# A chunked delta-rule recurrence inside a decoder trunk: inverting blocks of 32 tokens on VectorE instead of 16 on GpSimd

## The chip, the core and the metric

The kernel runs on one core of a Trainium2 chip. A core has five engines that run side by side, each with its own queue of instructions in program order: TensorE (PE, matmuls, with weight loads shown apart as PEld), VectorE (DVE), ScalarE (ACT), GpSimd (POOL) and SyncE (SP, which here issues all DMAs). They meet through semaphores. SBUF is the working memory of 128 partitions, PSUM the memory that matmuls write to. The metric is the time of one execution in microseconds on the device.

## What is computed

Two layers of a decoder trunk over 512 tokens of width 1024. In each layer one projection of x feeds four branches (a recurrence, causal attention, a convolution, cross-attention to a memory); each branch is gated, projected by its own w_o, merged under sigmoid gates, and a layer norm ends the layer. The change is in the recurrence (RWKV-7, 8 heads of 64):

```python
p = p + mu * (p_prev - p)
r, k, v, wl, al = jnp.split(p, (W, 2 * W, 3 * W, 3 * W + RWKV_LORA), axis=-1)
w_log = -jax.nn.softplus(-(w0 + jnp.tanh(wl) @ w2)) - 0.5
decay = jnp.exp(-jnp.exp(w_log.astype(jnp.float32)))
a = jax.nn.sigmoid(a0 + al @ a2)
...
def step(state, inp):
    r_t, w_t, k_t, v_t, a_t, b_t = inp        # a_t = -kk, b_t = kk * a
    sa = jnp.einsum('bhvk,bhk->bhv', state, a_t)
    state = (state * w_t[:, :, None, :] + sa[..., None] * b_t[:, :, None, :]
             + v_t[..., None] * k_t[:, :, None, :])
    return state, jnp.einsum('bhvk,bhk->bhv', state, r_t)
```

## The kernel before

**An order made ahead.** The class Plan keeps estimated clocks for the engines and lets generators ("tasks") take turns: a main stream of projections (weights are fetched in blocks of 512 KB, split by ScalarE and VectorE into a high and a low part, and multiplied in three passes) and side tasks, of which the recurrence's units are some. A task that yields "pe", "small", "late" or "ride" asks for a turn on TensorE; "small" and "late" collect work on 64x64 tiles so that TensorE changes its tile size seldom, and "ride" waits up to 4 us (RIDE) for such a visit of somebody else. A task that yields "slack" waits until VectorE's estimated queue is empty. The program is then issued in exactly that order, and every engine runs its own part of it in order. A matmul in float32 shows as two records in the trace.

**The recurrence.** A layer has four units (rwkv_unit, L839): two pairs of channel groups j0 times two halves of the tokens. A unit handles 8 chunks of 64 tokens for two heads at a time, on all 128 partitions. Its stages:

- *head* (L852 to L892): waits for `L["mids"] == un`, so that it starts when the unit before has passed its middle. z (decay and a, from the low-rank projections), tanh, the cumulative sum cum, exponentials D and E, and from them bt, kt, AR and w.
- *g* (L894 to L926): 64x64 matmuls that give the triangular matrix M of each chunk, key norms, and the masks' inputs. M is scaled and its four 16x16 diagonal blocks are packed into Mc.
- *substitution* (L931 to L968): Mc goes through DRAM (d1) into W, where each of 64 partitions holds one 16x16 block; GpSimd inverts all of them by 28 products and sums (ZT, tmpW); the result and its transpose go through DRAM (d2) into tc, zc and zq. That is 9 DMAs.
- meanwhile NQ, the bonus (bo, from r, k and v) and token-major copies of bt and kt (tokens, on TensorE); most of them yield "slack".
- *x0, x1, x2* (L1038 to L1104): three visits to 64x64 tiles. With T and Z, the inverted blocks spread to block-diagonal matrices, and M with its diagonal blocks removed (moff), x0 makes P and its transpose PT, x1 makes P·Z and P·P, which become QQ and PP, and x2 multiplies PP and QQ to the inverse Zi of the 64x64 matrix. x2 also holds the product of NQ and vt. A visit x0 also holds 32 other matmuls (x_0x or x_1x in the trace).
- *va, gb* (L1119 to L1164): the chunk's transition matrices Gs, H, B, Y0. `L["mids"]` counts up here.
- *state chain* (L1167 to L1190): three steps w of one product each, which "ride" in visits x0, x1 and x2 of the next unit; then yb, which may share the next unit's va.
- group norm and output.

rkv_items (L1256) puts the projections r, k, v of each channel group into the main stream in the order r0 k0 v0 r1 k1 v1; after v1 the two units of the pair are started.

L259 and L353 are the helpers through which VectorE, ScalarE and GpSimd operations and matmuls are issued, so most rows of the profile bear these lines; rows are told apart by tile names (x stands for x0, x1 and x2, g for g0 and g1). In the main stream ps_* and po are projections of 512 columns; mt and merged are VectorE's readers of po.

Of the kernel before, what the change touches and what calls it, by code (L numbers as in the profile page):

```python
# [10 lines left out]
F32 = mybir.dt.float32  # L11
# [5 lines left out]
ALU = mybir.AluOpType  # L17
# [30 lines left out]
for _n, _c in _PARTS:  # L48
# [6 lines left out]
    ("minc", 64), ("moff", 64), ("m16", 16), ("bm", 4), ("id2", 128),  # L55
# [169 lines left out]
class Engine:  # L225
# [5 lines left out]
    def __getattr__(self, name):  # L231
        f = getattr(self.eng, name)

        def call(*a, **k):
# [3 lines left out]
            for d in (o if name in ("activation", "copy") or self.key == "POOL" else i).shape[1:]:  # L238
                n *= d
# [93 lines left out]
def trunk_kernel(ctx: ExitStack, tc: tile.TileContext, A, out, dbg=None):  # L333
# [87 lines left out]
    scr = [[dp.tile([64 * (n + 1), 256], F32, tag=f"scr{n}{i}", name=f"scr{n}{i}").rearrange("a b -> (a b)") for n in range(2)] for i in range(2)]  # L421
# [24 lines left out]
    def params(l):  # L446
# [10 lines left out]
        om = cp.tile([128, 17], F32, tag="om", name=f"om{l}", bufs=2)  # L457
        V.tensor_scalar(out=om[:, 0:13], in0=prm[:, 0:13], scalar1=-1.0, scalar2=1.0, op0=ALU.mult, op1=ALU.add)
        ka = PCOL["k_a"]
        V.tensor_scalar(out=om[:, 13:17], in0=prm[:, ka:ka + 4], scalar1=-1.0, scalar2=1.0, op0=ALU.mult, op1=ALU.add)  # L460
        PRM[l] = prm, hp, om
# [247 lines left out]
    def layer_items(l):  # L709
# [67 lines left out]
        def begin_rwkv(get):  # L777
# [6 lines left out]
            L["blk"] = [L["rp"].tile([64] + n, F32, tag=x, name=x + t_) for x, n in (("W", [16, 16]), ("ZT", [2, 16, 16]), ("tmpW", [56]))]  # L784
# [11 lines left out]
            plan.spawn(parts())  # L796

# [15 lines left out]
        L["units"] = L["chains"] = L["mids"] = L["subs"] = L["read"] = L["fronts"] = L["backs"] = L["ends"] = 0  # L813
# [20 lines left out]

        def both(ap):

            return ap.rearrange("p s (c w) -> p (s c) w", w=64)

        def rwkv_unit(j0, hf, rkv):  # L839
# [3 lines left out]
            rr, kr, vr = ([x[n][:, cs] for x in rkv] for n in "rkv")  # L843
# [8 lines left out]
            yield lambda: L["mids"] == un  # L852
            th, ta = rk("s0", [2, 256], "th"), rk("s1", [2, 256], "ta")
            for s, j in js:
# [6 lines left out]
                S.activation(ta[:, s], z[:, 1, :], AF.Tanh, scale=0.5, bias=hp("a0", j))  # L861
# [3 lines left out]
            cum, kk, sq = rk("s2", [2, 256], "cum"), rk("s3", [2, 256], "kk"), rk("s5", [2, 256], "sq")  # L865
            for s, j in js:
                V.tensor_tensor_scan(out=cum[:, s], data0=reset, data1=th[:, s], initial=0.0, op0=ALU.mult, op1=ALU.add)
                S.activation(sq[:, s], kr[s], AF.Square, scale=pr("k_k", j))
                S.activation(kk[:, s], kr[s], AF.Copy, scale=pr("k_k", j))
# [4 lines left out]
            dl = rk("dl", [8, 1], bufs=2)  # L874
            S.copy(dl, D[:, :, 64:65])
            E = rk("s0", [2, 256], "E")
            S.activation(E, cum, AF.Exp)
            bt, kt, w = rk("bt", [2, 256]), rk("kt", [2, 256]), rk("s4", [2, 256], "w")
            V.scalar_tensor_tensor(out=bt, in0=ta, scalar=1.0, in1=kk, op0=ALU.add, op1=ALU.mult)
            V.scalar_tensor_tensor(out=bt, in0=bt, scalar=0.5, in1=E, op0=ALU.mult, op1=ALU.mult)  # L880
            for s, j in js:
                S.activation(w[:, s], ta[:, s], AF.Identity, scale=hp("k_a", j), bias=om[:, 13 + j:14 + j])
            yield
            AR = rk("AR", [2, 4, 2, 64])
            V.scalar_tensor_tensor(out=AR.rearrange("p s c m w -> p (s c) m w")[:, :, 0, :], in0=both(kk), scalar=-1.0, in1=D[:, :, 0:64], op0=ALU.mult, op1=ALU.mult)
# [3 lines left out]
            for s in SUB:  # L889
                V.tensor_tensor(out=w[:, s], in0=w[:, s], in1=kr[s], op=ALU.mult)  # L890
            V.tensor_tensor(out=kt, in0=w, in1=E, op=ALU.mult)
            yield  # L892

            g0, g1 = yield from pg.take([128, 2, 512], "g" + t, 2, soon)  # L894
# [26 lines left out]
            Mc = rk("zc", [8, 16], "Mc")  # L921
# [4 lines left out]
            d1, d2 = scr[un % 2]  # L926
            W, ZT, tmp = L["blk"]

            zt = []

            def substitution():  # L931
# [13 lines left out]
                for q in range(1, 15):  # L945
# [5 lines left out]
                    if q % 2:  # L951
                        yield
# [1298 lines left out]
```

## Time and profile before

| | |
|---|---|
| median of 3 runs | 1472.24 us (1472.14 to 1473.07) |
| the profiled execution | 1472.63 us, span 1470.8 us |
| TensorE busy / weight loads busy | 1458.1 us / 1227.7 us |
| VectorE, ScalarE, GpSimd busy | 1041.1, 682.8, 143.3 us |
| granted TensorE clock | 0.998 |

The span runs from the first to the last instruction; the execution's time is 1.8 us longer. Busy times count an instruction from start to end, and matmuls overlap, so TensorE's busy time is not its work; distances between the starts of matmuls are. In a row of a timeline the numbers are start and duration in us, then engine, line, operation, tiles out<-in, the shape and how many records were merged.

### The profile page before, as it was taken

Reading aid. Unit: us, or ns where it says so; the run is one execution under the profiler, and the core shown is the slowest. Engines: PE = TensorE matmul, PEld = TensorE weight load, DVE = VectorE, ACT = ScalarE, POOL = GpSimd, SP = SyncE. Lnnn points to the kernel's source line nnn. Section 1 sums busy time; section 2 is a strip of 40 time slices with the busy share of each in tenths; the row PEclk is TensorE's granted clock in tenths of the full one; section 3 lists DMA queues with packets and bytes.
Section 4 is the critical chain, followed back from the end, with each engine's and each line's share of the span. In section 5 each row is a group of like instructions: output and inputs, shape, how many; then the busy total and the mean of one; then the engine's idle time right before and its main releaser. Section 6 shows DMA issues by size and latency. Waiting matters only on the chain.

```text
span 1470.8 us, 28765 instructions
## 1 busy us (share of the span) xinstructions
PE 1458.1 (99%) x11673; PEld 1227.7 (83%) x11673; DVE 1041.1 (71%) x2025; ACT 682.8 (46%) x1331; POOL 143.3 (10%) x327
## 2 busy tenths in 40 slices
PE   9999999999999999999999999999999999999997
PEld 8888888888888888888999888888878888888886
DVE  6799997785756574655554899987867476756756
ACT  5556654436434444443264456633455444444331
POOL 0000000030201112100010000000030203030003
PEclk9999999999999999999999999999999999999999
DMA  6454333232232323333354152423232314132532
GB/s 220 126 145 105 93 110 99 86 84 95 82 90 81 92 75 97 99 127 125 112 165 123 61 147 68 133 88 101 88 104 61 112 47 126 51 108 90 193 95 83
DMA packets 90025, 154.03 MB, mean 105 GB/s; under 512 B 41634, under 2 KB 48034, under 8 KB 89892
## 3 DMA queue, kind: packets, MB, share of 16 engines
q1 hardware_dynamic: 89892, 152.19, 34.8%
q8 instruction: 92, 1.51, 0.4%
q14 instruction: 41, 0.34, 0.1%
HBM read 134.84 MB, written 5.78 MB: 96 GB/s over the span
## 4 chain that ended last, share of the span: by engine, by line
PE 96%; DVE 2%; ACT 1%; DMA 1%; issue 0%; SPq 0%; DVEq 0%; ACTq 0%
PE ps_m L353 23%; PE po L353 12%; PE pz L353 4%; PE ps_rg L353 3%; PE ps_cg L353 3%; PE ps_xg L353 3%; PE ps_r L353 3%; PE ps_v L353 3%; PE ps_xq L353 3%; PE ps_val L353 3%; PE ps_k L353 3%; PE ps_glu L353 3%; PE ps_mg L353 2%; PE ms L353 2%; PE pl L353 2%; PE x L353 2%
## 5 line engine op out<-in xcount | busy, mean ns | idle before, releaser
L259 DVE SCALAR_TENSOR_TENSOR cacc<-hpad,prm,cacc 128x512 f32<-128x512 f32 x240 | 178.9, 748 | 3.8
L259 ACT ACTIVATE tm<-ps_m,prm 128x512 f32<-128x512 f32 x64 | 44.0, 688 | 160.6 <-PE ps_m L353 160.4
L259 DVE SCALAR_TENSOR_TENSOR mt<-tm,po 128x512 f32<-128x512 f32 x48 | 33.0, 687 | 79.0 <-PE po L353 78.8
L259 POOL TENSOR_TENSOR ZT<-ZT,tmpW 64x14 f32<-64x14 f32 (+6 forms) x112 | 46.3, 413 | 8.8
L259 POOL TENSOR_SCALAR ZT<-W 64x256 f32<-64x256 f32 x8 | 5.7, 718 | 408.3 <-DMA W<-scr 296.0
L259 ACT ACTIVATE mP<-ms,nmm 128x128 f32<-128x128 f32 (+3 forms) x64 | 33.7, 529 | 21.0 <-DVE nmm L259 16.2
L259 POOL TENSOR_TENSOR tmpW<-ZT,W 64x14 f32<-64x14 f32 (+6 forms) x112 | 39.6, 353 | 8.2
L259 DVE TENSOR_TENSOR merged<-merged,mt 128x512 f32<-128x512 f32 x48 | 33.4, 697 | 1.6
L259 POOL MEMSET D<- 128x8 f32 x8 | 0.9, 115 | 336.9 <-DVE mP L259 158.3
L259 DVE CUSTOM_DVE_ANT_0 ms<-ms,causal 128x128 f32<-128x128 f32 (+3 forms) x64 | 31.1, 499 | 0.5 <-PE ms L353 0.2
L259 ACT COPY mPT<-mt 128x128 f32<-128x128 f32 (+3 forms) x64 | 26.4, 428 | 5.2 <-PE mt L358 4.9
L358 PE MATMUL mt<-cst,mP 128*128 128x128 f32 x160 | 26.8, 274 | 0.4 <-ACT mPT L259 0.4
L259 DVE TENSOR_SCALAR mP<-mP,smm 128x128 f32<-128x128 f32 (+3 forms) x64 | 24.8, 387 | 2.4
L358 PEld LDWEIGHTS mt<-cst,mP 128*128 128x128 f32 x160 | 20.2, 140 | 6.8 <-issue 0.9
L259 POOL TENSOR_SCALAR lrs<-lmv 128x1 f32<-128x1 f32 x8 | 4.4, 550 | 220.1 <-DVE lmv L259 215.4
L259 ACT ACTIVATE yb<-yb,mr,gr 128x64 f32<-128x64 f32 x64 | 22.1, 430 | 0.0
L353 PE MATMUL ms<-kTl,qT 96*128 96x128 f32 (+3 forms) x64 | 21.5, 336 | 0.0
L259 DVE SCALAR_TENSOR_TENSOR merged<-tm,po 128x512 f32<-128x512 f32 x16 | 11.0, 686 | 14.0 <-PE po L353 14.0
L259 POOL TENSOR_SCALAR gr<-gm 128x8 f32<-128x8 f32 x8 | 3.2, 396 | 180.6 <-DVE gm L259 180.6
L353 PE MATMUL ms<-kTh,qTl 96*128 96x128 f32 (+3 forms) x64 | 20.6, 322 | 0.0
L353 PE MATMUL ms<-kTh,qT 96*128 96x128 f32 (+3 forms) x64 | 20.5, 321 | 0.0
L259 ACT ACTIVATE xP<-xs,nmx 128x256 f32<-128x256 f32 x32 | 15.2, 474 | 11.2 <-DVE nmx L259 11.2
(3585 smaller groups left out, 5213.0 us busy)
## 6 DMA issues: line engine op xcount, KB each, us to landing
w<-in_w_ch_dram SPq DMA_DIRECT2D x146, 512.0 KB, 3.6
w<-in_w_o_dram SPq DMA_DIRECT2D x32, 512.0 KB, 3.6
w<-in_w_out_dram SPq DMA_DIRECT2D x16, 512.0 KB, 3.5
w<-in_w_lat_dram SPq DMA_DIRECT2D x15, 336.0 KB, 2.9
w<-in_w_mk_dram SPq DMA_DIRECT2D x8, 512.0 KB, 3.5
w<-in_w_mv_dram SPq DMA_DIRECT2D x8, 512.0 KB, 3.9
w<-in_w_qk_dram SPq DMA_DIRECT2D x8, 320.0 KB, 3.5
mr<-in_memT_dram SPq DMA_DIRECT2D x8, 256.0 KB, 5.5
```

Source lines behind the costliest of these rows:

```text
L259: return self.plan.keep(f(*a, **k))
L353: plan.keep(nc.tensor.matmul(o, lhsT, rhs, start=start, stop=stop))
L358: plan.keep(nc.tensor.transpose(o, i, ident))
```

## The change

1. The block that is inverted directly is 32 tokens wide, made of two 16-wide inverses and one product between them. VectorE does it: `solve` inverts the 16x16 blocks in place by doubling (2, 4, 8), then two more products give the off-diagonal 16x16 block (ax, bc). POOL's ZT and tmpW go. The blocks Mo beside the diagonal take their own way through DRAM (dm). The DMAs are twelve instead of nine.
2. moff now removes 32-wide blocks, so one factor is enough: x0 makes PP from M and tt (the transposed inverse, made by a VectorE transpose), 32 columns wide; x1 multiplies PP with Zd and also holds the product of NQ and vt. x2 is gone, with P, PT, Q, QQ and T.
3. The head waits for `L["heads"] == un`, which the unit before sets after its x0, and it stops for `L["mids"] == un` only before kt, sq and AR. Step w of the state chain may go on from the next unit's g (`L["goes"]`), and the second step waits for its x0. w moves to the shared pool u of 32 buffers; kk is not stored, its factors are in om (8 more columns).
4. r and k of both channel groups are projected before v, and the units start after the second k; the bonus and the transposes of v wait for v (`spoken`). Several "slack" yields are gone. Transposes of v come before x0 instead of after it.
5. Setup: two DMAs fill the unused half of a scratch tensor with zeros, and a constant bm2 is added.

The diff's core:

```diff
+            if l == 0:
+                for x in scr:
+                    DMA(rows(x[2])[1], zero)
...
-            yield lambda: L["mids"] == un
-            th, ta = rk("s0", [2, 256], "th"), rk("s1", [2, 256], "ta")
+            yield lambda: L["heads"] == un
+            th, w = rk("PT", [2, 256], "th"), u("w" + t).rearrange("p (s w) -> p s w", s=2)
...
-            V.scalar_tensor_tensor(out=bt, in0=ta, scalar=1.0, in1=kk, op0=ALU.add, op1=ALU.mult)
-            V.scalar_tensor_tensor(out=bt, in0=bt, scalar=0.5, in1=E, op0=ALU.mult, op1=ALU.mult)
+            for s, j in js:
+                V.scalar_tensor_tensor(out=bt[:, s], in0=kr[s], scalar=om[:, 21 + j:22 + j], in1=E[:, s], op0=ALU.mult, op1=ALU.mult)
+            V.scalar_tensor_tensor(out=bt, in0=w, scalar=1.0, in1=bt, op0=ALU.add, op1=ALU.mult)
...
+            yield lambda: L["mids"] == un
+            kt, sq, AR = rk("kt", [2, 256]), rk("s5", [2, 256], "sq"), rk("AR", [2, 4, 2, 64])
+            for s, j in js:
+                V.scalar_tensor_tensor(out=AR[:, s, :, 0, :], in0=kr[s].rearrange("p (c w) -> p c w", c=4), scalar=om[:, 17 + j:18 + j], in1=D[:, 4 * s:4 * s + 4, 0:64], op0=ALU.mult, op1=ALU.mult)
...
+            L["goes"] += 1
...
+            V.tensor_scalar(out=Mo, in0=M8[:, :, 16:32], scalar1=bm[:, 0:1], scalar2=None, op0=ALU.mult)
+            V.scalar_tensor_tensor(out=Mo, in0=M8[:, :, 48:64], scalar=bm[:, 2:3], in1=Mo, op0=ALU.mult, op1=ALU.add)
...
+                for i in range(2):
+                    DMA(W[32 * i:32 * i + 32, 0:256], pairs(d1)[i], f"W{i}" + t)
...
+                yield from solve()
+                plan.due(W)
+                yield
+                DMA(ax[:, 0], W[0:32, 0:256], "a0" + t)
+                DMA(bc[:, 0], W[32:64, 0:256].unsqueeze(1).to_broadcast([32, 4, 256]), "b0" + t)
+                for i, d in enumerate((dl_, dr)):
+                    DMA(pairs(d)[i], W[32 * i:32 * i + 32, 0:256])
...
+                for x, y, c in ((0, 1, 1), (1, 2, 0)):
+                    for i in range(2):
...
+                        V.tensor_tensor(out=pr[i], in0=src.unsqueeze(2).to_broadcast([128, 2, 16, 16]),
+                                        in1=by.unsqueeze(1).to_broadcast([128, 2, 16, 16]), op=ALU.mult)
+                    for i in range(2):
+                        V.tensor_reduce(out=ax[:, y].rearrange("p (r k) -> p r k", k=16)[:, 2 * i:2 * i + 2], in_=pr[i], axis=AX.X, op=ALU.add)
+                    yield
...
+                DMA(rows(dr)[0], ax[:, 2])
...
+                DMA(zq[:, :, 0:16], dl_.rearrange("(e p t) -> p e t", e=8, t=16), "z0" + t)
+                DMA(zq[:, :, 16:32], dr.rearrange("(e p t) -> p e t", e=8, t=16))
...
+            def solve():
+
+                w3 = W[:, 0:256].rearrange("p (r c) -> p r c", c=16)
+                w4 = W.rearrange("p (i x) -> p i x", x=68)
+                V.memset(W[:, 0:256:17], 1.0)
+                t8 = ax[0:64, 2, 0:8].rearrange("p (i c) -> p i c", i=4)
+                for o, x, y in (...):
+                    V.tensor_tensor(out=t8, in0=x.to_broadcast([64, 4, 2]), in1=y.to_broadcast([64, 4, 2]), op=ALU.mult)
+                    V.tensor_tensor(out=o, in0=o, in1=t8, op=ALU.add)
...
+                for n in (4, 8):
...
+                    for step in range(2):
+                        for i, x, y in zip(at, us, ps):
...
+                            V.tensor_tensor(out=y, in0=src.unsqueeze(2).to_broadcast([64, n, n, n]),
+                                            in1=by.rearrange("p k c -> p c k").unsqueeze(1).to_broadcast([64, n, n, n]), op=ALU.mult)
+                        for i, x, y in zip(at, us, ps):
+                            V.tensor_reduce(out=w3[:, i:i + n, i + n:i + 2 * n] if step else x, in_=y, axis=AX.X, op=ALU.add)
...
+                plan.due(Mo)
+                yield
+                DMA(dm.rearrange("(c p t) -> p c t", c=8, t=16), Mo)
+                plan.due(dm)
+                yield
+                DMA(bc[:, 1], pairs(dm)[0].unsqueeze(1).to_broadcast([32, 4, 256]))
...
+            tt = rk("tt", [8, 32])
+            V.transpose(out=tt.rearrange("p e t -> p (e t)"), in_=zq.rearrange("p e t -> p (e t)"))
...
-            for q, a, b in ((0, M, T), (1, T, M)):
-                for s in SUB:
-                    for cp, c2, h in quads:
-                        MM(x0[HALF[h], q, s, c2, cp], a[HALF[c2], s, 2 * h + cp], b[HALF[c2], s, 2 * h + cp], start=True, stop=True, four=True)
+            for s in SUB:
+                for h, cp, c2 in quads:
+                    MM(x0[HALF[c2 ^ cp], c2, 2 * s + h], M[HALF[c2], s, 2 * h + cp], tt[HALF[c2], s, 2 * h + cp], start=True, stop=True, four=True)
...
-            for q, a, b in ((0, P, Zd), (1, PT, P)):
-                for s in SUB:
-                    for cp, c2, h in quads:
-                        MM(x1[...], a[HALF[h], s, 2 * cp + c2], b[HALF[h], s, 2 * cp + c2], start=True, stop=True, four=True)
...
-                    MM(x2[HALF[h], 0, s, c2, cp], PP[HALF[c2], s, 2 * h + cp], QQ[HALF[c2], s, 2 * h + cp], start=True, stop=True, four=True)
+                    MM(xz[HALF[h], s, g, cp], PP[HALF[g], cp, 2 * s + h], Zd[HALF[g], cp, 2 * s + h], start=True, stop=True, four=True)
             for s in SUB:
                 for cp, c2, h in quads:
-                    MM(x2[HALF[h ^ cp], 1, s, c2, h], NQ[s][HALF[c2], 2 * h + cp, 0], vt[s][HALF[c2], 2 * h + cp], start=True, stop=True, four=True)
+                    MM(xq[HALF[h ^ cp], s, c2, h], NQ[s][HALF[c2], 2 * h + cp, 0], vt[s][HALF[c2], 2 * h + cp], start=True, stop=True, four=True)
...
-            yield lambda: L["chains"] == un and (un == 3 or L["fronts"] > un + 1)
+            yield lambda: L["chains"] == un and (un == 3 or L["goes"] > un + 1)
...
+                    if len(states) == 3 - hf and un < 3:
+                        yield lambda: L["fronts"] > un + 1
...
-                    if n == "v" and j % 2:
+                    if n == "k" and j % 2:
                         for hf in range(2):
-                            plan.spawn(rwkv_unit(j - 1, hf, rkv[j - 1:j + 1]))
+                            plan.spawn(rwkv_unit(j0, hf, rkv[j0:j0 + 2]))
...
-            for i, n in enumerate("rkv"):
+            for i, n, j in (0, "r", 0), (1, "k", 0), (0, "r", 1), (1, "k", 1), (2, "v", 0), (2, "v", 1):
```

More of the change, by code (lines that the diff above doesn't have):

```diff
@@ L237, in call @@
             n = 1
-            for d in (o if name in ("activation", "copy") or self.key == "POOL" else i).shape[1:]:
+            for d in (o if name in ("activation", "copy", "memset") or self.key == "POOL" else i).shape[1:]:
                 n *= d
@@ L2074, in layer_items @@
         ch_item(12, "wlal", wlal, lambda: "lora" in L)
-        for j in range(4):
+        for j in (0, 2):
             rkv_items(j)
```

197 lines of the change are left out of this document (103 added, 94 removed).

## The prediction

> **What bounds the kernel now.** I read the page first: busy shares, then the chain that ended last.
>
> ```profile
> PE 1458.1 (99%) x11673; PEld 1227.7 (83%) x11673; DVE 1041.1 (71%) x2025; ACT 682.8 (46%) x1331; POOL 143.3 (10%) x327
> ...
> PE 96%; DVE 2%; ACT 1%; DMA 1%; issue 0%; SPq 0%; DVEq 0%; ACTq 0%
> ```
>
> TensorE (PE) is busy in 99% of the 1470.8 us span, and 96% of the chain is its own queue. A busy share can hide waits, so I went on to the view of who waited for whom, for PE alone.
>
> ```profile
> PE x L353 <- issue: 0.9, 2, 0.5
> ...
> PE bo L353 <- DVE rbl L259: 0.4, 1, 0.4
> PE cqs L353 <- DVE cql L259: 0.4, 1, 0.4
> PE pl L353 <- DVE w2l L259: 0.3, 1, 0.3
> PE pmv L353 <- DVE w124l L259: 0.2, 1, 0.2
> ```
>
> VectorE (DVE) cost PE 0.4 + 0.4 + 0.3 + 0.2 = 1.3 us in the whole run. So the recurrence's latency is covered by other projections, and only what PE itself issues counts. What a visit to the recurrence costs PE is read from start times in the timeline; this is the visit that the change removes (x2 of the first unit):
>
> ```profile
> 347.95 0.39 PE L353 MATMUL ps_m<-xh,w58l 128*128 128x512 f32 x1
> 348.27 0.69 PE L353 MATMUL x<-QQ,PP 64*64 64x64 f32 x32
> 348.78 0.65 PE L353 MATMUL x<-vt,NQ 64*64 64x64 f32 x32
> 349.36 0.50 PE L353 MATMUL po<-yxg0l,w59h 128*128 128x512 f32 x1
> 349.70 0.39 PE L353 MATMUL po<-yxg0h,w59h 128*128 128x512 f32 x1
> ```
>
> The 512-column matmuls start every 0.23 us although each row says 0.39: they overlap, so distances between starts are the price. From 347.95 to 349.70 are 1.75 us, in which two large matmuls (0.23 each) also ran: the visit costs 1.75 - 0.46 = **1.29 us**. Each record x32 is 16 float32 matmuls of two records; two such groups take 2 x 0.47 = 0.94, so going to 64x64 tiles and back costs 0.35.
>
> [...]
>
> **The change, part by part.**
>
> *Factors instead of powers.* With 16-wide blocks a unit needs P and PT (x0), two products with them (x1) and a last product (x2): five groups of 16 matmuls. With 32-wide blocks one factor is left: x0 has one group, now 32 columns wide, and x1 has one group and the NQ.vt group that was in x2. Eight units (four in each of two layers):
>
> ```profile
> L353 PE MATMUL x<-M,T x256: 218/218/218, 340.8 to 1314.9; 64*64 64x64 f32 x128
> ```
>
> 256 records are 8 units of 32. In x0 one group goes; its price between starts:
>
> ```profile
> 340.76 0.65 PE L353 MATMUL x<-M,T 64*64 64x64 f32 x32
> 341.23 0.41 PE L353 MATMUL x_0x<-AR,bt 64*64 64x64 f32 x16
> ```
>
> that is 0.47 us. x1 keeps two groups. x2 goes as a visit, 1.29 us. Per unit 0.47 + 1.29 = 1.76, times eight = **-14.1 us**.
>
> The other x0 group shrinks from 64 to 32 columns. The trace has no 32-column matmul; the nearest rows are 64 columns (0.47) and 1 column:
>
> ```profile
> 296.66 0.59 PE L353 MATMUL g<-cst,sq 64*64 64x1 f32 x32
> 297.10 1.08 PE L353 MATMUL g_0x<-AR,kt 64*64 64x128 f32 x32
> ```
>
> 0.44 us for a group of one column. So between nothing and 8 x 0.03 = 0.2 us is saved; I take nothing. [...] A price in proportion to columns would add 8 x 0.24 = 1.9 us of gain; I keep that for the low end.
>
> *Rides.* State steps w ride in visits of the next unit; with x2 gone they are to ride in g, x0 and x1. One costs, from its start to the large matmul after it:
>
> ```profile
> 1324.20 0.41 PE L353 MATMUL w<-S,Gs 64*64 64x64 f32 x8
> 1324.54 0.50 PE L353 MATMUL ps_rg<-xl,w214h 128*128 128x512 f32 x1
> ```
>
> 0.34 less the return of about 0.1: the same in any visit, so nothing. A step that misses its visit pays one of its own, 0.35. Six of the 18 change their host (three rides in each of six unit pairs, the first now in g): from nothing to 6 x 0.35 = 2.1, or 18 x 0.35 = 6.3 if all miss. I take nothing, since g of the next unit now starts only after the unit's own gb has been read, as the first step does.
>
> *x1 stalls.* A few x1 visits break in the middle:
>
> ```profile
> 345.21 0.46 PE L353 MATMUL x<-P,PT 64*64 64x64 f32 x16 [0.35 <-issue]
> ```
>
> The waits view has 0.9 us of it in all. It may stay or go; I count nothing and keep 0.9 for the low end.
>
> *The inversion moves from GpSimd to VectorE.* No row shows solve() itself; these are the nearest forms:
>
> ```profile
> L259 DVE TENSOR_REDUCE nmx<-xs 128x1 f32<-128x256 f32 x32 | 13.4, 418 | 0.2
> ...
> L259 DVE BATCH_NORM_STATS2 gs<-yb 128x6 f32<-128x64 f32 x64 | 9.2, 210 | 0.0
> ...
> L259 DVE SCALAR_TENSOR_TENSOR Mc<-M,cst,Mc 128x128 f32<-128x128 f32 x24 | 8.4, 352 | 0.8
> ...
> L259 DVE SCALAR_TENSOR_TENSOR w<-r,prm,w 128x256 f32<-128x256 f32 x16 | 7.4, 486 | 0.0
> ...
> L259 DVE TENSOR_TENSOR QQ<-x,Q 128x512 f32<-128x512 f32 x8 | 5.5, 687 | 5.8 <-PE x L353 5.8
> ...
> L259 DVE RECIPROCAL rn<-s 128x4 f32<-128x4 f32 x16 | 1.9, 163 | 0.3
> ```
>
> Removed per unit: T, QQ, PP, one bt, one AR, five operations of 512 at 0.69 = 3.4 us. Added: memset and four tiny ones at 0.16 = 0.8; eight of 64 elements at 0.21 = 1.7; twelve of 512 (products and reductions; a reduction of 256 takes 418 ns, so 512 is near 687) = 8.2; Mo 0.6; two halves each of PP, bt and AR, at 0.42 to 0.49, 2.8; the 32x32 transpose, 256 elements, 0.4. Sum 14.5, **net +11 us per unit, 89 us in the run** (DVE 71% to about 77%). None of it is on PE's chain as long as VectorE still empties PSUM and splits weights in time. The cover:
>
> ```profile
> 280.00:600.00 320.00, 318.79 (x3568) 262.06 (x3567) 207.62 (x396) 145.88 (x287) 56.52 (x139) 1.00 0.30 85
> ```
>
> ```profile
> L259 DVE SCALAR_TENSOR_TENSOR mt<-tm,po 128x512 f32<-128x512 f32 x48 | 33.0, 687 | 79.0 <-PE po L353 78.8
> ```
>
> In layer 0's recurrence VectorE works 207.6 of 320 us; four units add 44, 79%. At the tightest reader, po, it idled 79 us before 48 operations: it came first and waited for PE. A split weight is ready about 10 us ahead:
>
> ```profile
> 321.05 1.23 DVE L259 TENSOR_TENSOR w57l<-w,w57h 128x1024 fp32r<-128x1024 f32 x1
> ...
> 331.75 0.39 PE L353 MATMUL ps_m<-xl,w57h 128*128 128x512 f32 x1
> ```
>
> If the cover fails: solve and the two products queue VectorE work in four runs of 2.5 to 2.8 us per unit, 32 in the run. A po caught behind one is read up to 2.8 + 0.7 us late, and its PSUM buffer is needed 12 x 0.23 = 2.7 us later: 0.7 us of PE per run, at most 32 x 0.7 = 22 us. Bounds 0 and 22. Nearest row: all of today's VectorE waits, 1.3 us; I take as much again, **+1.3**.
>
> *DMAs.* The step issues twelve small DMAs instead of nine on SP's queue, where weights queue too, with one more round trip through DRAM (and two zero fills once). Today's waits there:
>
> ```profile
> SPq L365 <- DVE Mc L259: 83.0, 8, 14.2
> ```
>
> Weights already sat behind waits of up to 14.2 us without PE noticing. VectorE takes POOL's place as the one waited for; below 14 us nothing changes. Cost 0, upper end inside the 22 above.
>
> *Head ahead, r and k ahead of v.* The head begins with its z matmuls:
>
> ```profile
> L353 PEld LDWEIGHTS zw<-lxw,lhw x16: 187/188/188, 279.9 to 1264.1; 128*128 128x128 f32 x16
> ```
>
> From 279.9 to the first g (sq at 296.66, above) are 17 us, which now lie beside the unit before. The z matmuls, bo and the transposes are the same in number; exponentials, cum, bt and w only run earlier, beside the other unit. This shortens the recurrence, not PE's work. Nothing is gained, since PE has no hole at the end of the recurrence; nothing is lost except that VectorE's work is packed closer, which is the risk above. v now comes last: v0 and v1 are 48 matmuls of 0.23, 11 us, less than the first head's 17, so bo's PSUM bank, which is held until v is there, is not held longer. w takes one of the 32 shared buffers per unit; a wait for it could hold ScalarE's tanh and what stands behind it, but a unit ahead there is room: nothing, and at most part of the 22. The removed ScalarE copies (46% busy) and the few setup operations count nothing.
>
> **Sum.** The profiled execution took 1472.63 us (span 1470.8 and 1.8 around it), 0.4 above the median of 1472.24. 1472.6 - 14.1 + 1.3 = 1459.8, so **1460**.
>
> **Rivals.**
> 1. *Rides miss.* Steps or yb make visits of their own: 2.1 to 6.3 us back, 1462 to 1466. For it: the timetable is estimated ahead. Against: the rows quoted above, where they ride.
> 2. *VectorE becomes the bound inside the recurrence* (the slower side). Four units in 320 us are 80 us each; with the head's 17 us gone they are 63, and 207.6 + 44 us of VectorE work have 252 us: full. po is then late after nearly each run: +22, **1480**. It decides from (14.1 + 2.9) / 32 = 0.53 us per run. Against: the idle 79 us at mt, PE's 1.3 us of waits, and that part of the 207.6 belongs to the other projections and shrinks with the stretch.
> 3. *No change*: with weight loads at 83% PE had room and something else sets the pace, so the time stays at 1472; or about half of the 22 us and some missed rides give the gain back. 1470 to 1475.
> 4. *The move up is what counts*: the recurrence's end was what PE waited for, and the 17 us of each head count too, at least in part. Against: the waits view has no such wait. Below 1455.
>
> **How the numbers follow.** Forecast (1455 to 1464) 0.62; missed rides and small VectorE losses (1464 to 1469) 0.14; no change 0.10; slower 0.10; more than forecast 0.04. Low end: 1459.8 less 1.3, 1.9 and 0.9 is 1455.7, so 1455. High end: the 22 us at half, 1459.8 - 1.3 + 11 = 1469.5, and a share of the missed rides, 1471; that leaves out the slower case and the cases below 1455, and part of no change. About 0.2% (2.9 us) is what a measurement of this kernel can tell from no change; so faster 0.80, same 0.10, slower 0.10.
>
> **What would show it.** Right: x falls from 192 records a unit (six rows like the one quoted) to 96; one visit to 64x64 tiles fewer in each unit, with w still riding in the others; PE's VectorE waits under 3 us; DVE near 1130 us; POOL down by the ZT and tmpW rows. Wrong: starts of po more than 0.23 us apart with mt as releaser, w visits alone, or weights late behind SP's new waits.

## The result, and the profile after

| | before | after |
|---|---|---|
| median | 1472.45 us (1472.14 to 1473.07, 4 runs) | 1462.68 us (1461.68 to 1465.0, 4 runs) |
| the profiled execution | 1472.63 us, span 1470.8 | 1465.0 us, span 1463.2 |
| visits to 64x64 tiles, time in them | 51, 101.4 us | 44, 89.1 us |

The ratio is 0.9935, 95% interval [0.9918, 0.9953]: faster by 10 us, with 1460 predicted. The last row of the table was counted over the starts of TensorE's matmuls, as the prediction did for one visit; in the profiled execution of e0, below, it is 44 visits and 87.7 us.

The page of after, its busy shares and its chain:

```profile
PE 1446.8 (99%) x10905; PEld 1218.1 (83%) x10905; DVE 1128.7 (77%) x2261; ACT 672.1 (46%) x1275; POOL 44.9 (3%) x79
...
PE 90%; DVE 5%; ACT 1%; DMA 1%; issue 1%; SPq 0%; DVEq 0%; ACTq 0%
```

TensorE is as busy as before and still the bound, but VectorE has come up to 77%, and its share of the chain from 2% to 5%. The x tiles of after, by tile (count of records, duration, first and last start):

```profile
L353 PE MATMUL x<-tt,M x256: 219/219/241, 324.9 to 1295.9; 64*64 64x32 f32 x128
...
L353 PE MATMUL x<-Zd,PP x256: 218/218/267, 329.3 to 1299.3; 64*64 64x64 f32 x128
...
L353 PE MATMUL x<-vt,NQ x256: 218/218/218, 329.8 to 1299.7; 64*64 64x64 f32 x128
```

Three rows of 256 records are 96 a unit, half of the 192 before. Two visits of the second unit in the timeline (start, duration):

```profile
394.55 0.67 PE L353 MATMUL x<-tt,M 64*64 64x32 f32 x32
395.04 0.44 PE L353 MATMUL x_1x<-AR,bt 64*64 64x64 f32 x16
...
399.28 0.69 PE L353 MATMUL x<-Zd,PP 64*64 64x64 f32 x32
399.80 0.65 PE L353 MATMUL x<-vt,NQ 64*64 64x64 f32 x32
400.26 0.41 PE L353 MATMUL w<-S,Gs 64*64 64x64 f32 x8
400.61 0.50 PE L353 MATMUL ps_r<-xl,w66h 128*128 128x512 f32 x1
```

The group of 32 columns takes 395.04 - 394.55 = 0.49 us, no less than one of 64. The state step w rides in x1, as it was to; all 18 steps found a host.

Who PE waited for in after (total, times, longest, in us):

```profile
PE gb_1x L353 <- issue: 2.1, 1, 2.1
PE bo L353 <- DVE rbl L259: 1.7, 1, 1.7
PE cqs L353 <- DVE cql L259: 1.0, 1, 1.0
PE pl L353 <- ACT xh L259: 1.0, 1, 1.0
PE warm L353 <- PEq L2312: 0.8, 1, 0.8
PE x L353 <- DVE PP L259: 0.6, 1, 0.6
PE mt L358 <- ACT mPT L259: 0.4, 1, 0.4
PE ps_m L353 <- DVE mt L259: 0.4, 1, 0.4
PE pq L353 <- ACT xql L259: 0.3, 1, 0.3
PE ps_r L353 <- DVE mt L259: 0.2, 1, 0.2
PE ps_cg L353 <- DVE mt L259: 0.2, 1, 0.2
```

The waits for VectorE are 1.7 + 1.0 + 0.6 + 0.4 + 0.2 + 0.2 = 4.1 us, against 1.3 before, and more than the under 3 us that the prediction gave as a sign of being right; a hole of 2.1 us in gb_1x waits for nothing that the profile shows. VectorE in after, by form, and its busy time in layer 0's recurrence (the third busy time of the window, whose columns are those of the prediction's window):

```profile
L259 DVE SCALAR_TENSOR_TENSOR mt<-tm,po 128x512 f32<-128x512 f32 x48 | 32.8, 684 | 63.7 <-PE po L353 62.9 <-issue 0.6
L259 DVE TENSOR_TENSOR pr<-ax,bc 128x512 f32<-128x512 f32 x32 | 32.4, 1055 | 0.0
L259 DVE TENSOR_REDUCE ax<-pr 128x32 f32<-128x512 f32 x32 | 20.4, 679 | 0.0
...
L259 DVE TENSOR_TENSOR pw<-ax,W 64x512 f32<-64x512 f32 x8 | 8.4, 1049 | 0.3
```

```profile
280.00:600.00 320.00, 319.36 (x3254) 263.21 (x3253) 257.10 (x543) 143.36 (x267) 10.78 (x17) 1.00 0.33 92
```

VectorE's busy time there rose from 207.62 to 257.10 of 320 us (the third of the bracketed counts is its own: 396 instructions became 543). At the tightest reader, mt, its idle time fell from 79.0 to 63.7 us: less cover, but cover.

### The profile page after: what moved, and what is told of

Read it like the earlier page. It is cut to its first block, busy times and chain, and to the rows that moved or that the text cites. A ratio compares the mean times of both kernels' runs of the same rounds, so it can differ in the third digit from the quotient of the medians.

```text
span 1463.2 us, 27202 instructions
## 1 busy us (share of the span) xinstructions
PE 1446.8 (99%) x10905; PEld 1218.1 (83%) x10905; DVE 1128.7 (77%) x2261; ACT 672.1 (46%) x1275; POOL 44.9 (3%) x79
## 4 chain that ended last, share of the span: by engine, by line
PE 90%; DVE 5%; ACT 1%; DMA 1%; issue 1%; SPq 0%; DVEq 0%; ACTq 0%
PE ps_m L353 22%; PE po L353 11%; PE pz L353 4%; PE ps_cg L353 3%; PE ps_xg L353 3%; PE ps_xq L353 3%; PE ps_val L353 3%; PE ps_rg L353 3%; PE ps_mg L353 3%; PE ps_r L353 3%; PE ps_glu L353 3%; PE ps_v L353 2%; PE ps_k L353 2%; PE ms L353 2%; PE pl L353 2%; PE ps_mk L353 1%
## 5 line engine op out<-in xcount | busy, mean ns | idle before, releaser
L259 DVE SCALAR_TENSOR_TENSOR mt<-tm,po 128x512 f32<-128x512 f32 x48 | 32.8, 684 | 63.7 <-PE po L353 62.9
L259 DVE TENSOR_TENSOR pr<-ax,bc 128x512 f32<-128x512 f32 x32 | 32.4, 1055 | 0.0
L358 PEld LDWEIGHTS mt<-cst,mP 128*128 128x128 f32 x160 | 20.2, 140 | 6.9 <-issue 0.9
L259 ACT ACTIVATE Zd<-zq,cst 64x128 f32<-64x128 f32 (+1 forms) x48 | 19.2, 400 | 3.6 <-DMA zq<-scrr 2.9
L259 DVE TENSOR_REDUCE ax<-pr 128x32 f32<-128x512 f32 x32 | 20.4, 679 | 0.0
L259 DVE TENSOR_TENSOR z<-z,pz 128x256 f32<-128x256 f32 (+1 forms) x19 | 8.2, 432 | 15.7 <-PE pz L353 15.5
L353 PE MATMUL mo<-mPT,v 128*64 128x128 f32 x320 | 19.2, 275 | 0.0
L353 PEld LDWEIGHTS mo<-mPT,v 128*64 128x64 f32 x320 | 17.3, 137 | 2.3 <-issue 1.1
```

The source lines that it names most:

```text
L259: return self.plan.keep(f(*a, **k))
L353: plan.keep(nc.tensor.matmul(o, lhsT, rhs, start=start, stop=stop))
L358: plan.keep(nc.tensor.transpose(o, i, ident))
```

## Experiments

Theory A: the gain is TensorE's own issue time (14.1 us predicted), of which some 4 us are given back. Theory B: the head and r, k moved up are what helps. For the part given back there were several candidates: the planner's wrong price for the strided products, the dropped "slack" yields, the amount of VectorE's work, and the hole. Eleven kernels were made from after, and after itself was run again beside them. Ratios are to the kernel before on the same chip. In e5, e10 and e11 every instruction that is left stands in the order of after, by the traces; in the other edits the planner made a new order, and its price is part of the difference.

| run | edit | median, us | ratio, 95% interval |
|---|---|---|---|
| e0_after_again | none | 1461.85 | 0.9927 [0.9915, 0.9939] |
| e1_head_late | head waits for mids again | 1463.91 | 0.9938 [0.9926, 0.9951] |
| e2_v_in_order | r k v order of before | 1466.01 | 0.9957 [0.9944, 0.9969] |
| e3_old_pe_work | old number of matmuls and visits | 1478.14 | 1.0034 [1.0022, 1.0046] |
| e4_priced | planner knows the real price | 1483.91 | 1.0075 [1.0062, 1.0088] |
| e5_contiguous | stride moved from product to reduction | 1462.07 | 0.9928 [0.9914, 0.9941] |
| e6_slack | "slack" yields back | 1477.98 | 1.0033 [1.0020, 1.0045] |
| e7_twice | products written twice | 1487.64 | 1.0102 [1.0088, 1.0116] |
| e8_one_visit | only the visit x2 put back | 1471.27 | 0.9988 [0.9979, 0.9996] |
| e9_gpsimd | half the products on GpSimd | 1468.77 | 0.9969 [0.9957, 0.9981] |
| e10_shifted | 51 matmuls more at the start | 1462.09 | 0.9932 [0.9919, 0.9944] |
| e11_half | half the products left out | 1460.33 | 0.9917 [0.9903, 0.9931] |

**The kernel after, unchanged.**

> The changed kernel once more, unchanged, as the base for the runs beside it. Median 1462 to 1463.5 (four runs gave 1461.7 to 1465.0). If the 2.1 us stop in gb with its slow clock after it, seen in the first profile, belongs to the program, it is there again at the same matmuls; if it was an accident of that execution, the span is about 1460.

1461.85 us, the yardstick of the differences below. bo waits 1.7 us again, cqs 0.9 and gb_1x 1.3: these waits belong to the order of the program, not to one execution, though their size varies.

### TensorE's own work

**All of it put back.** e3 adds matmuls that nobody reads: a second group in x0 and a visit x2 of two groups in each unit, so that records are 11673 as before.

```diff
+            xd = x0[:, :, 128:384].rearrange("p c (e w) -> p c e w", e=4)
...
+                    MM(xd[HALF[c2 ^ cp], c2, 2 * s + h], M[HALF[c2], s, 2 * h + cp], M[HALF[c2], s, 2 * h + cp], start=True, stop=True, four=True)
...
+            x2, = yield from pg.take([128, 2, 512], "x2" + t, 1, soon)
...
+                    MM(za[HALF[h], s, g, cp], PP[HALF[g], cp, 2 * s + h], PP[HALF[g], cp, 2 * s + h], start=True, stop=True, four=True)
...
+                    MM(zb[HALF[h ^ cp], s, c2, h], NQ[s][HALF[c2], 2 * h + cp, 0], vt[s][HALF[c2], 2 * h + cp], start=True, stop=True, four=True)
```

> The changed kernel with TensorE's old number of groups: one more group of 16 matmuls in x0 and a visit of its own with two groups (32 matmuls) between x1 and va, none of them read. Theory A: 8 x (0.47 + 1.29) = 14.1 us more than the changed kernel, 1476 to 1478, that is slower than the kernel before by what VectorE gives back, 3 to 6 us. Theory B: only the added latency counts, under 1468.

1478.14 us, 16.3 above e0: theory A. Counted over starts as in the table above, e3 spends 103.2 us in its visits and e0 87.7, so 15.5 of the 16.3 are TensorE's own time. It also gives the other half of the account. With TensorE's matmuls as many as before, VectorE's work as after and the new order, the kernel is 1478.1 - 1473.2 = 4.9 us slower than before (ratio 1.0034, interval above 1). So in these runs the change is a gain of 16.3 us on TensorE and a loss of 4.9; 1.8 of the loss lies in the visits themselves (103.2 us against 101.4 before).

**Only the visit.** e8 is e3 without xd.

> The kernel after with one TensorE visit per unit put back and nothing else: after the x1 visit stands a visit x2 of two groups of 16 small matmuls whose results nobody reads (the second x0 group stays away). Theory A (what counts is what TensorE issues; the visit is worth 1.29 us and the x0 group 0.47 us per unit, times eight): +10.3 us against the unchanged kernel after (1461.9), so 1470 to 1474, ratio to before about 0.998 to 1.001, visits to 64x64 tiles up by eight, about 10 us more in them. The earlier run with visit and group together lost 16.3 us, so by A the difference to that run is 3.8 us. Rival (what the visit costs is the lengthening of the recurrence, not the issue time): PE's waits for VectorE or for the end of the recurrence grow by several us and the time lies above 1475; or, if the visit were hidden, below 1466.

1471.27, 9.4 above e0, where the visit alone was put at 10.3. The visits take 97.2 us, 9.5 more than in e0, and PE's waits stayed as they were (bo 1.8, cqs 1.0), so the visit costs its own issue time and not a longer recurrence. The second x0 group is the rest, 16.3 - 9.4 = 6.9, against 3.8 by its matmuls; the waits for VectorE and the holes without a releaser in e3 (mt 1.4 us, x 0.8 + 0.8) are part of the difference, and the two runs stand beside different sets of runs of before (1473.2 and 1473.0).

### What was moved up

**Head late again.**

```diff
-            yield lambda: L["heads"] == un
+            yield lambda: L["mids"] == un
```

> The head waits again for the middle of the unit before. Theory A (TensorE's own work made the gain): units take some 15 us longer each, the time stays within 1.5 us of the changed kernel, 1461 to 1464. Theory B (the shorter recurrence made it): most of the gain goes, 1468 or more. Theory C (packed VectorE work gives part back): 1 to 3 us faster than the changed kernel, since the same work is spread over more time.

1463.91, 2.1 above e0, with intervals that overlap. PE's largest wait is a new one:

```profile
PE po L353 <- DVE yrg2l L259: 2.3, 1, 2.3
```

yrg2l is an operand of the projection that reads the recurrence's output: in e1 the recurrence's end in layer 1 is late by this much.

**r, k, v in the order of before.**

```diff
-        for i, n, j in (0, "r", 0), (1, "k", 0), (0, "r", 1), (1, "k", 1), (2, "v", 0), (2, "v", 1):
+        for i, n, j in (0, "r", 0), (1, "k", 0), (2, "v", 0), (0, "r", 1), (1, "k", 1), (2, "v", 1):
...
-                if n == "k" and j % 2:
+                if n == "v" and j % 2:
```

> Projections in the old order r k v r k v, units started after the second v. Theory A: no change against the changed kernel, 1461 to 1464. Theory B: the recurrence starts 11 us later, in each of two layers, and some of it is lost: 1466 or more.

1466.01, 4.2 above e0, the intervals apart. That is just inside the range of theory B, but 4.2 us are not most of a gain of 11. The same wait of 2.3 us for yrg2l, and 1.8 for merged. So these two parts are not the gain, but they aren't nothing: with them the end of the recurrence stays off TensorE's path.

### What is given back

**The planner's price.** Plan reckons a product of 512 elements at 0.6 us; with a strided operand it takes 1.05. e4 tells it the truth; only the order changes.

```diff
+            elif name == "tensor_tensor" and len(i.shape) == 4 and i.shape[-1] <= 16:
+                c = 132 + 1.79 * n
```

> Same operations; only the order made ahead reckons the products of the inversion with what they take (0.13 us + 1.79 ns per element, 1.05 us for 512) and not 0.60. Theory C1 (VectorE gives back about 4 us because the order places bo, cqs and readers of po on a VectorE that is later than reckoned): TensorE's VectorE waits fall from some 4 us to under 2, time 2 to 3 us under the changed kernel, 1458.5 to 1460.5. Theory C2 (VectorE is too full, whatever the order): waits of the same size at other places, 1461 to 1463.

1483.91, 22 us worse, a clear miss. The waits of e4 and its timeline around the recurrence's end in layer 1 (the bracket is PE's idle time before the row and its releaser):

```profile
PE ty L360 <- ACT yb L261: 7.0, 4, 6.5
PE ps_xq L355 <- ACT w147h L261: 4.7, 1, 4.7
PE ps_r L355 <- DVE mt L261: 2.6, 1, 2.6
```

```profile
1363.11 0.69 PE L355 MATMUL yb<-S,B 64*64 64x64 f32 x32
1370.27 0.48 PE L360 MATMUL ty<-cst,yb 128*128 128x128 f32 x1 [6.47 <-ACT yb L261]
...
1375.99 0.50 PE L355 MATMUL po<-yrg2l,w220h 128*128 128x512 f32 x1 [0.73 <-DVE yrg2l L261]
```

```profile
1368.00:1376.00 8.00, 4.44 (x11) 2.49 (x11) 3.37 (x9) 3.99 (x10) 1.15 (x1) 0.57 0.48 164
```

yb is the last product of the recurrence, ty its transpose. In e4 the last ty starts at 1372.3 us, in after at 1337.4 (1334.6 in e0, 1357.7 before). Between them no projection is left in TensorE's order; it waits 6.5 us for ScalarE, and over the 8 us that hold the end of this wait the granted clock is 0.57 (the number after the bracketed counts in the window); its po rows start 0.43 us apart from 1372.96 to 1374.67, and 0.23 behind 1376.33. Two more operands are late elsewhere (w147h at 866 us, where no recurrence runs). TensorE's waits are 19.3 us in all, 7.5 in e0, and the mean granted clock is 0.992 instead of 0.999, by this share an estimated 10 us of the span of 1480.7: together that is the 22 us. A truer price changed the whole order, for the worse.

**"slack" again.** NQ, the bonus's products, M8 and rbl yield "slack" as before, so they give way to other VectorE work.

```diff
-            yield
             for s in SUB:
+                yield "slack"
                 V.tensor_tensor(out=NQ[s].rearrange("p (h a) m w -> p h a (m w)", h=2), in0=gvs[s],
...
+            yield "slack"
             V.tensor_tensor(out=M8, in0=M8, in1=cc("moff").unsqueeze(1).to_broadcast([128, 8, 64]), op=ALU.mult)
-            yield
...
             for s, j in js:
+                yield "slack"
                 V.scalar_tensor_tensor(out=w[:, s], in0=rr[s], scalar=pr("r_k", j), in1=w[:, s], op0=ALU.mult, op1=ALU.mult)
             S.copy(rbh, w)
-            yield
+            yield "slack"
             V.tensor_tensor(out=rbl, in0=w, in1=rbh.bitcast(F32), op=ALU.subtract)
```

> NQ, w, M's mask and rbl yield to VectorE's queue again, as in the kernel before. If packing of these is what makes readers of po late, the mt waits go (0.8 us) and 1 to 2 us are gained; C1 says that bo and cqs still stand on a wrong price, so under 1 us.

1477.98, 16.1 above e0, where a gain was expected. The same end as in e4: the last ty at 1366.1, a mean clock of 0.994, and

```profile
PE ty L358 <- ACT yb L259: 7.5, 4, 6.9
```

**More VectorE work.** e7 writes each off-diagonal product twice.

```diff
+                        for again in range(2):
                         V.tensor_tensor(out=pr[i], in0=src.unsqueeze(2).to_broadcast([128, 2, 16, 16]),
```

> The four products of the off-diagonal block are written twice with the same result: 8 x 4 x 1.05 = 34 us more on VectorE, of which the order knows 0.60 each. If VectorE were the bound inside the recurrence (rival 2), each of the 34 us would cost up to one: 1475 or more. If it is cover with few collisions (forecast), 0.05 us for each, as 4 us for 88: 1463 to 1466.

1487.64, 25.8 us more for 34 us of VectorE work (66.5 - 32.4 in the rows of pr), in the range of rival 2 and not of the forecast. The longest waits of e7:

```profile
PE ps_m L353 <- DVE mt L259: 4.8, 3, 2.0
PE ps_cg L353 <- DVE w200l L259: 3.7, 1, 3.7
PE x L353 <- DVE PP L259: 2.1, 4, 0.8
```

PE's waits for VectorE are 20.1 us in all, 4.6 in e0. mt before ps_m is PSUM read late, w200l a weight split late: both mechanisms of rival 2, in one view. But the run does not show that the amount of work is what costs. The planner reckoned the second products and made a new order: 260 of VectorE's 2261 instructions of after stand elsewhere in it, as do 320 in e4, which added no work and lost 22 us. And w200l was late behind a VectorE that stood idle (timeline of e7):

```profile
1237.96 0.69 DVE L259 SCALAR_TENSOR_TENSOR cacc<-ctn,cacc 128x512 f32<-128x512 f32 x1 [1.62 <-ACT ctn L259]
...
1239.77 1.22 DVE L259 TENSOR_TENSOR w200l<-w,w200h 128x1024 fp32r<-128x1024 f32 x1
```

w200h was ready at 1236.56, while VectorE idled 1.62 us for ctn; w200l stood behind that in its queue.

**Less VectorE work.** e11 leaves every second product out, with the order of all the other instructions unchanged.

```diff
+                        if i:
+                            plan.op("DVE", 65 + 1.04 * 512, _names(pr[i]), _names(ax, bc))
+                            continue
...
-... in_=pr[i], axis=AX.X, op=ALU.add)
+... in_=pr[0], axis=AX.X, op=ALU.add)
```

> The kernel after with 16 of the 32 products of the off-diagonal blocks left out (the second reduction reads the first product, so half of each factor block is not the reference's); every other instruction stands in the same order on every engine. VectorE is relieved of 16 times 1.05 us, 16.9 us (1128.7 to about 1112), with nothing moved to another engine. Theory D (the 4 to 5 us given back against the removed TensorE work come from the amount of VectorE's work): 1457 to 1460, waits for VectorE (4 us) at 2 us or less, recurrence's last ty a few us earlier. Rival E (they are single late operands at fixed places of the order, such as rbl before bo and cql before cqs, which less work between does not move, with the late instructions and the slower clock behind them): 1461 to 1463, with bo and cqs still waiting 1.7 and 1.0 us.

1460.33, 1.5 below e0 for 14 us less (busy 1128.7 to 1114.3): 0.1 us for each. The intervals of the two ratios overlap, so the 1.5 is not clear of noise. cqs no longer waits; bo does:

```profile
PE bo L353 <- DVE rbl L259: 1.7, 1, 1.7
```

The time lies between the ranges of D and E and decides neither: cqs went and the last ty came 2.5 us earlier (1332.1) as D has it, bo stayed as E has it. Nor does it bound what VectorE's work costs: only 14 of the 88 us that the change added are gone, and at 0.1 us for each all 88 would come to 9, more than the whole loss.

**Half the products on GpSimd**, the same relief without leaving anything out.

```diff
-                        V.tensor_tensor(out=pr[i], in0=src.unsqueeze(2).to_broadcast([128, 2, 16, 16]),
+                        (V, G)[i].tensor_tensor(out=pr[i], in0=src.unsqueeze(2).to_broadcast([128, 2, 16, 16]),
```

> The kernel after with every second product of the off-diagonal blocks (16 of 32 in the run, 1.05 us each on VectorE) made by GpSimd, beside VectorE's other half. VectorE is relieved of 16.9 us (1128.7 to about 1112), with the same results. Theory D (the 4 to 5 us given back are VectorE's crowding, at 0.05 to 0.76 us of time per us of its work): 1457 to 1461, with the waits for VectorE (rbl, cql, mt, PP; 4.1 us) at 2 us or less. Rival E (they come from single queue positions and latencies, not from the amount of VectorE's work): 1461 to 1464, waits of the same sum at other places. Rival F (GpSimd's product takes 2 us or more, or slows VectorE beside it, and the recurrence gets later): above 1464.

1468.77, 6.9 above e0: rival F, with a new order as part of it. By tile and in the timeline of e9:

```profile
L259 POOL TENSOR_TENSOR pr<-ax,bc x16: 1526/1680/4453, 307.0 to 1292.8; 128x512 f32<-128x512 f32 x16
L259 DVE TENSOR_TENSOR pr<-ax,bc x16: 1035/1053/2412, 310.3 to 1292.6; 128x512 f32<-128x512 f32 x16
```

```profile
306.93 3.48 DVE L259 SCALAR_TENSOR_TENSOR cacc<-hpad,prm,cacc 128x512 f32<-128x512 f32 x3
306.96 2.11 POOL L259 TENSOR_TENSOR pr<-ax,bc 128x512 f32<-128x512 f32 x1 [140.38 <-DMA ax<-W]
```

A GpSimd product takes 1.5 to 4.5 us, and VectorE beside it is held up: three cacc take 3.48 us instead of 3 x 0.75, one of them alone 1.92. VectorE's busy time fell by 3.6 us only, not by 16.9. VectorE's own products took up to 2.41 us, with a median of 1.05, and cacc was stretched as above, while the reductions stayed at 674 to 687 ns, three of them wholly beside a GpSimd product. What the two engines get in each other's way over, the run does not show.

**Where the stride stands.** In e5 the product reads and writes with step 1, and the reduction that follows it reads with a step of 16 elements; the products of solve are changed in the same way.

```diff
-                        by = bc[:, c].rearrange("p (k w) -> p w k", k=16)
-                        V.tensor_tensor(out=pr[i], in0=src.unsqueeze(2).to_broadcast([128, 2, 16, 16]),
+                        by = bc[:, c].rearrange("p (k w) -> p k w", k=16)
+                        V.tensor_tensor(out=pr[i], in0=src.unsqueeze(3).to_broadcast([128, 2, 16, 16]),
...
-... in_=pr[i], axis=AX.X, op=ALU.add)
+... in_=pr[i].rearrange("p r k w -> p r w k"), axis=AX.X, op=ALU.add)
```

> The products' second operand is read with step 1 instead of step 16 (or n), and the reduction reads with a step instead. If the step of a product's operand makes 1.05 us of 0.69, products fall to about 0.69, reductions stay at 0.68 or rise to 1.05. If they stay, VectorE is busy 17 us less, about 1112 us, and by C1 (the reckoned 0.60 is then nearer) 1 to 2.5 us are gained; if reductions rise by as much, nothing changes.

1462.07, no difference. VectorE's rows of e5 say why:

```profile
L259 DVE TENSOR_REDUCE ax<-pr 128x32 f32<-128x512 f32 x32 | 31.9, 1040 | 0.0
L259 DVE TENSOR_TENSOR pr<-ax,bc 128x512 f32<-128x512 f32 x32 | 20.6, 685 | 0.0
```

The product fell from 1055 to 685 ns, the reduction rose from 679 to 1040: the price goes where the stride goes. The step of 16 elements costs 0.36 to 0.37 us for 512 elements in either place.

**The hole.** In after it lies inside a run of 64x64 matmuls:

```profile
1158.06 0.28 PE L353 MATMUL gb_1x<-VA,BP 64*64 64x64 f32 x4
1160.42 0.27 PE L353 MATMUL gb_1x<-VA,BP 64*64 64x64 f32 x2 [2.08 <-issue]
```

```profile
1156.00:1160.00 4.00, 2.34 (x124) 2.20 (x121) 2.81 (x10) 2.04 (x4) 0.00 (x0) 1.00 0.71 271
1160.00:1166.00 6.00, 5.58 (x50) 4.52 (x50) 4.45 (x11) 3.45 (x6) 0.00 (x0) 0.72 0.02 5
```

It falls on the moment when weights arrive at 271 GB/s (last number), and the clock behind it is 0.72: it is 0.50 for 3.4 us from 1162.0 on, in which the large matmuls start 0.43 us apart instead of 0.23. In e0, behind the hole of 1.3 us, it stays full:

```profile
1159.00:1165.00 6.00, 5.79 (x58) 4.88 (x58) 4.66 (x11) 3.79 (x7) 0.00 (x0) 1.00 0.02 5
```

e10 splits the 17 warm-up matmuls into 68 of a quarter of the columns; all else keeps its order, 51 matmuls further on.

```diff
-        MM(warm[:, 0:256], ones[0], ones[1], start=True, stop=True)
+        for q in range(3):
+            plan.keep(nc.tensor.matmul(warm[:, 64 * q:64 * q + 64], ones[0], ones[1][:, 0:64], start=True, stop=True))
...
+        plan.keep(nc.tensor.matmul(warm[:, 192:256], ones[0], ones[1][:, 0:64], start=True, stop=True))
```

> The kernel after, with the 17 warm-up matmuls of 256 columns at the start issued as 68 of 64 columns: the same columns, the order of everything else unchanged on every engine; each later TensorE instruction stands 51 matmuls (with their weight loads) further on in the program. Theory H (the hole of 1.3 to 2.1 us in gb_1x, which waits for nothing the profile shows, is TensorE's instruction stream arriving late, in blocks): the hole leaves its matmuls, moves by some 51 matmuls or goes, and with it the slow clock behind it; 1458 to 1462. Rival (it hangs on the data or on the transfers at that moment): the hole of over 1 us stays at the same matmuls of gb_1x, 1461 to 1464. At most 1 us may be lost at the start in either case.

The matmuls of that visit now follow each other without a break; another gb_1x breaks for 0.5 us. So the hole doesn't belong to these matmuls or their data. The run alone can't tell whether their place in the program moved it, or that the visit came 1.3 us later (gb starts at 1157.16, in after at 1155.85) beside the same transfers. The DMA records say more. The profile calls two queues instruction; this is the larger, in after and in before (packets, MB, share):

```profile
q8 instruction: 86, 1.41, 0.4%
...
q8 instruction: 92, 1.51, 0.4%
```

Its packets are of 16 KB, and there is one for each 128 matmuls begun: 86 for the 10905 matmuls of after, 90 for 11417 in e8, 92 for 11673 in before and e3. In after one of them lands at 1158.96 us and TensorE goes on at 1160.42; in e0 at 1157.91 and 1159.21; in e10, at its new place, at 1306.24 and 1307.52. In all the traces there are 21 holes of over 150 ns before a matmul that no releaser explains, and every one ends 1.2 to 1.6 us after such a packet has landed, though the packets come 17 us apart on average. That fits theory H, TensorE waiting for its instructions; the traces show the times, not what a packet holds. Of the large matmuls, 128 last 29 us; in the window above 124, most of them small, were done in 2.34 us of busy time. Most packets land without a hole (86 packets and one hole in after, 92 and three in before); why there is one at some of these places and not at others is not shown.

The time is 1462.09, the same as e0: the profiled execution has 1.1 us more at the start (pl, for w2l) and 0.6 more for mt (1.0 against 0.4), which outweigh the 0.8 us that the hole lost. So moving the hole gained nothing that the median shows.

## Why the prediction held, and where it did not

- **TensorE's own issue time, -14.1 us: right.** Visits went from 101.4 to 89.1 us; without TensorE's idle time in them, 1.1 us before and 2.7 after, that is -13.9. The experiments put the two parts back for 16.3 us together and 9.4 for the visit (10.3 predicted). There are 44 visits, not 43, since one yb that shared a visit now stands alone (0.35 us).
- **32 columns save nothing: right.** 0.49 us for the group, beside 0.47.
- **Rides: right.** All 18 steps rode. Six in g, six in x0, five in x1 and one in va.
- **VectorE +89 us: right in sum, wrong in its terms.** 1041.1 + 89 = 1130, measured 1128.7. But the term "twelve of 512", 8.2 us per unit, took the products at 0.69 where the strided ones take 1.05: four of pr and two of pw are 6 x 0.36 = 2.2 us more a unit. That much of the rest was reckoned too dear.
- **Its price, +1.3: too small.** The waits for VectorE grew by 4.1 - 1.3 = 2.8 us, not 1.3, and by e3 the whole loss is 4.9. "As much again" as the present waits was a guess from the nearest row. That the sum came within 3 us of the result is in part luck: by e3 the gain was put 2.2 us too low and the loss 3.6 too low, and the two errors work against each other. How near rival 2 (1480) was is open: e7 shows the waits that it named, but in a new order.
- **x1 stalls, 0.9, not counted.** They went: no x visit of after has a hole without a releaser. Its first x1 visit is long for another reason, a late PP:

```profile
329.31 0.69 PE L353 MATMUL x<-Zd,PP 64*64 64x64 f32 x32 [0.65 <-DVE PP L259]
```

In their place came the hole in gb_1x, 2.1 us in after with a low clock behind it, 1.3 in e0 without one. By the DMA records it looks like the same thing at another place: the two stalls of before, too, end 1.3 and 1.4 us after an instruction packet has landed. No step foresaw it. Outside the visits, the stretches of over 150 ns beyond the even distance of starts grew from 6.1 to 10.4 us, which include the waits for VectorE and the slow clock. -12.3 in the visits and +4.3 outside make -8.0; the profiled executions differ by 7.6.
- **DMAs cost nothing: right.** SP waited longer (Mc up to 20.2 us, in the row below), beyond the 14 us that the prediction had taken as safe, and yet PE's waits behind the start name no weight.

```profile
SPq L365 <- DVE Mc L259: 94.5, 11, 20.2
```

- **Head ahead, r and k ahead: "nothing is gained" was too simple.** No time is gained by a shorter recurrence as such, so rival 4 fell. But they are cover: without the one the time was 2.1 us longer (within the intervals), without the other 4.2, new orders included. The prediction looked for a hole at the recurrence's end in before and found none; it did not ask how near to one the end was. What seems to count is how much of the span is left behind the last ty: 126 us in after and e0, without a wait; 113 in before, still without; 113 and 111 in e1 and e2, with 2.3 us; 110 and 108 in e6 and e4, with some 7 us and a slow clock. So before stood about at the edge, with the two parts the end lies 13 us away from it, and without either of them it is back.

What stays open is where the 5 us that are given back come from. By the starts of e3, 1.8 of them lie in the visits and 3.2 outside (9.3 us against 6.1 in before). What part of this is the amount of VectorE's work, and how much more of it the kernel would bear, no run shows: e11 is not clear of noise, and e7 and e9 changed the order too. The 1.7 us of bo and the hole are single places of the order; no run removed them both. No version beat after by more than the measurement tells: e5 and e10 are equal to it, and e11, which leaves work out, is within the intervals.

## What to carry to other kernels

Where TensorE is the bound and its starts are evenly spaced, count what it issues: matmul groups and changes of tile size, at the distance between starts, were worth what the count said. Paying for such a gain with another engine's time had a price even though that engine had room: 88 us more on VectorE came with a loss of some 5. In a kernel whose order is planned ahead, an edit that touches the planner's prices, yields or work is a new order, which alone cost up to 22 us here; what a part is worth should be tested with the order of everything else held fixed.

## What the runs showed of the hardware

- 512 float32 elements on VectorE took 1.04 to 1.06 us where an operand had a step of 16 elements and 0.68 to 0.69 where it had not, in a product (1.055 in after, 0.685 in e5) and in a reduction (1.040 in e5, 0.679 in after) alike.
- On the larger queue that the profile calls instruction, packets of 16 KB landed, one for each 128 matmuls begun (86 with 10905 matmuls, 90 with 11417, 92 with 11673). In or just behind dense runs of small matmuls, for the most part, TensorE stood for up to 2.1 us with no releaser in the profile, and each of these 21 holes ended 1.2 to 1.6 us after such a packet had landed.
- Behind some pauses of TensorE the granted clock was lower: 0.72 for the 6 us behind the hole of 2.1 us in after, 0.57 in the 8 us that hold the end of a wait of 6.5 us in e4. Behind others it was not: behind the hole of 1.3 us in e0 it was 1.00, and so it was behind bo's wait of 1.7 us in after. Where it was lower, large matmuls started 0.43 us apart instead of 0.23, so the time lost there was more than the wait. What sets the clock the runs do not show.
